# Gate and up projection of a SwiGLU part turned channel-major, in an encoder layer on one Trainium2 core

## The chip, the core and the metric

The kernel runs on one core of one Trainium2 chip. The metric is the time of one execution on the device, in microseconds. The engines are named TensorE (PE in the rows, PEld for its weight loads), VectorE (DVE), ScalarE (ACT), GpSimd (POOL) and SyncE (SP, which starts most DMAs).

## What is computed

One layer of a bidirectional encoder: 272 tokens (16 learned ones before 256) of width 2048 go through four token mixers, fed by one combined input projection, and then through a SwiGLU feed-forward part with 5632 hidden channels. The change is in the feed-forward part, for the 256 tokens that are kept:

```python
def rms_norm(x, gain):
    y = xf * lax.rsqrt(jnp.mean(xf * xf, axis=-1, keepdims=True) + EPS)
    return (y * gain.astype(F32)).astype(x.dtype)

def swiglu(n, w_gate, w_up, w_down):
    return (jax.nn.silu(n @ w_gate) * (n @ w_up)) @ w_down
...
        h = h + swiglu(rms_norm(h, norm_ffn[l]), ffn_w_gate[l], ffn_w_up[l], ffn_w_down[l])
    return rms_norm(h, norm_final)[:, N_META:]
```

All inputs are float32. The kernel splits each operand of a large product into a high part, which the faster matmul type of float32 holds, and the low part that is left; a product is then three matmuls: high by high, high by low, low by high.

## The kernel before

The work is a long run of matmuls over weights that stream in once. Every weight piece is 128 partitions of 1024 numbers (512 KB). `piece` (line 131) starts its DMA from SP into one of four `raw` buffers, lets ScalarE write the high part `hi` (line 152) and VectorE the low part `lo` (line 155), each into one of three buffers. The order of the pieces is the order in which the host has packed them (`pack`, line 1191).

There are two forms of matmul, named here by which operand is held in the array.

- `xs_gemm` (line 164) holds the tokens: 128 tokens by 128 input channels are the weights of the array, and 512 output channels of a weight piece move. Its results lie with tokens on the partitions: two accumulators (one for each 128 tokens) of 512 channels. A piece is 2 row blocks of 128 by 512 columns, and a piece does 12 matmuls (lines 178 to 180).
- `mix_chunk` (line 355), in the mixing part of the program, holds the weights: 128 by 128 of a piece are held and 272, 258 or 256 tokens move. Its results lie with channels on the partitions: two accumulators (one for each 128 channels). A piece is 4 row blocks by 256 columns, and does 24 matmuls (lines 364 to 366).

Both take their accumulators from one pool of four (`accp`).

The feed-forward part starts after the output projection. There, for each quarter `d` of the channels, `turn` (line 1034) transposes the residual stream `hh` on TensorE, ScalarE writes `n2h` and VectorE `n2l`: the input with channels on the partitions, times the norm's gain. The norm's other factor, one number per token (`rstd`), isn't in it: `sumsq` and `norm` (lines 1018, 1022) make it beside, and it is multiplied in behind the gate and up products. Work of this kind is put into a list `later`, and a product that starts emits the list after its first pieces: after 24 matmuls in the gate product (`at=4`, line 1058).

The hidden channels are done in 11 parts of 512, in two halves of 6 and 5 (`GU_HALF`): 6 parts, 1 part of the second half, the down product of the first half (`down(0, ...)`), the 4 other parts, the down product of the second. `gate_up` (line 1057) does a part: two `xs_gemm` calls, for each 128 tokens a silu with `rstd` as the scale on ScalarE (line 1070) and a product on VectorE (line 1071) that takes the up result times `rstd` times the silu. Tokens are on the partitions there, so `rstd` is one number per partition. The down product wants the hidden channels on the partitions, so each 128 by 512 result is transposed by 4 matmuls with the identity (line 1064, out of `later` in the product that follows), and `split` (line 199) makes `hidh` on ScalarE and `hidl` on VectorE out of it.

The order of each engine's queue is set by the framework's scheduler, from the order of the code, its own estimate of times and a priority that draws the preparation of pieces ahead.

Of the kernel before, what the change touches and what calls it, by code (L numbers as in the profile page):

```python
# [10 lines left out]
F32 = mybir.dt.float32  # L11
F32R = mybir.dt.float32r
U8 = mybir.dt.uint8
AF = mybir.ActivationFunctionType
# [3 lines left out]
P = 128  # L18
D = 2048
SEQ = 256  # L20
# [5 lines left out]
KT = D // P  # L26
# [4 lines left out]
GU_HALF = (6, 5)  # L31
# [38 lines left out]
def body(tc, a, out):  # L70
    nc = tc.nc
    V, G, A, PE = nc.vector, nc.gpsimd, nc.scalar, nc.tensor
    MUL, ADD, SUB = ALU.mult, ALU.add, ALU.subtract
# [7 lines left out]
    accp = pool("acc", 4, space=PSUM)  # L81
    psp = pool("ps", 4, space=PSUM)

    def ps(name="ps", shape=(P, 512)):
        return psp.tile(list(shape), F32, tag="ps", name=name)
# [7 lines left out]
    ident = const.tile([P, P], F32, name="ident")  # L93
# [37 lines left out]
    def piece(kt, cols, dst=None, skip=0):  # L131

        beside()
        i = wpos[0]
        wpos[0] += 1
        with tc.high_priority(offset=WAHEAD if i >= 6 else 0):
            raw = rawp.tile([P, kt, cols], F32, tag="raw", name="raw")
            nc.sync.dma_start(raw, a["w"][i].rearrange("p (k n) -> p k n", k=kt))
            if dst:
                hi, lo = dst  # L140
            else:
                hi, lo = [p.tile([P, 1024 + WPAD], F32R, tag=x, name=x)[:, skip:skip + 1024]
                          .rearrange("p (k n) -> p k n", k=kt) for p, x in ((hip, "hi"), (lop, "lo"))]
            if i < NPOOL:
                for j in range(kt):
                    ins = G.tensor_scalar(hi[:, j], raw[:, j], 1.0, 0.0, op0=MUL, op1=ADD)  # L146
                    if "G" in last:
                        after(ins, last["G"])
                    ins = G.tensor_tensor(lo[:, j], raw[:, j], hi[:, j].bitcast(F32), op=SUB)  # L149
                    last["G"] = ins  # L150
            else:
                ins = A.copy(hi, raw)  # L152
                if i in behind:
                    after(ins, behind[i][0])
                ins = V.tensor_tensor(lo, raw, hi.bitcast(F32), op=SUB)  # L155
                if i in behind:
                    after(ins, behind[i][1])
            if i == 1:
                first.append(ins.ins)
        return hi, lo  # L160

    later = []

    def xs_gemm(xh, xl, kts, at=2):


        acc = [accp.tile([P, 512], F32, tag="acc", name=f"acc{t}") for t in range(2)]
        n = len(kts)
        for i in range(0, n, 2):
            if i == at:  # L170
                while later:
                    later.pop(0)()
            wh, wl = piece(2, 512)
            for j in range(2):
                k = kts[i + j]
                for t in range(2):
                    s = slice(t * P, t * P + P)
                    PE.matmul(acc[t], xh[:, k, s], wh[:, j], start=(i + j == 0), stop=False)  # L178
                    PE.matmul(acc[t], xh[:, k, s], wl[:, j], start=False, stop=False)  # L179
                    PE.matmul(acc[t], xl[:, k, s], wh[:, j], start=False, stop=(i + j == n - 1))  # L180
        return acc
# [17 lines left out]
    def split(hi, lo, src):  # L199
        A.copy(hi, src)  # L200
        V.tensor_sub(lo, src, hi.bitcast(F32))

    def rsqrt(dst, ssum, scale):

        V.tensor_scalar(dst, ssum, scale, EPS, op0=MUL, op1=ADD)
        A.activation(dst, dst, AF.Sqrt)
        V.reciprocal(dst, dst)
# [5 lines left out]
    def half(name):  # L213
        return gp.tile([P, 512], F32, tag="half", name=name)
# [55 lines left out]
    def quarter(g, q):  # L270
        return xts[g][q // 2][:, q % 2 * 512:q % 2 * 512 + 512]
# [25 lines left out]
    for t in range(2):  # L297
        for q, e in enumerate("AVAV"):
            dump = H("dump", 512)
            x, acc = quarter(t, q), ss[:, t, q:q + 1]  # L300
# [21 lines left out]
    for k in range(KT):  # L322
        pt = ps("ptn")
        for t in range(2):
# [3 lines left out]
                                         op0=MUL, op1=SUB)]  # L328
# [683 lines left out]
    n2h = np_.tile([P, KT, SEQ], F32R, tag="nh", name="n2h")  # L1012
    n2l = np_.tile([P, KT, SEQ], F32R, tag="nl", name="n2l")
    ssum = const.tile([P, 2, 2, 4], F32, name="ssum")
    rstd = const.tile([P, 2, 2], F32, name="rstd")
    hh = {}

    def sumsq(i, t, d):
        dump = half("dump")
        A.activation(dump, hh[t, d], AF.Square, accum_out=ssum[:, i, t, d:d + 1])  # L1020

    def norm(i):
        V.tensor_reduce(rstd[:, i], ssum[:, i], op=ADD, axis=mybir.AxisListType.X)
        rsqrt(rstd[:, i], rstd[:, i], 1.0 / D)

    for d in range(4):
        acc = xs_gemm(mth, mtl, range(KT))
        for t in range(2):
            h = half("h")
# [16 lines left out]
        later.extend([lambda d=d: turn(d, 0), lambda d=d: turn(d, 1)])  # L1046
        for t in range(2):
            later.append(lambda t=t, d=d: sumsq(0, t, d))
    later.append(lambda: norm(0))
    ph1.close()  # L1050


    hid_p = pool("hid")
    hidh = [hid_p.tile([P, 4 * n, SEQ], F32R, tag=f"hid{i}h", name=f"hidh{i}") for i, n in enumerate(GU_HALF)]
    hidl = [hid_p.tile([P, 4 * n, SEQ], F32R, tag=f"hid{i}l", name=f"hidl{i}") for i, n in enumerate(GU_HALF)]

    def gate_up(part, c):
        ag = xs_gemm(n2h, n2l, range(KT), at=4)
        au = xs_gemm(n2h, n2l, range(KT))

        def turn(t, s):
            pt = ps("pth")
            for j in range(4):
                PE.transpose(pt[:, j * P:j * P + P], s[:, j * P:j * P + P], ident)  # L1064
            o = (slice(None), slice(4 * c, 4 * c + 4), slice(t * P, t * P + P))
            split(hidh[part][o], hidl[part][o], pt.rearrange("p (k n) -> p k n", k=4))

        for t in range(2):
            s = half("silu")
            A.activation(s, ag[t], AF.Silu, scale=rstd[:, 0, t:t + 1])  # L1070
            V.scalar_tensor_tensor(s, au[t], rstd[:, 0, t:t + 1], s, op0=MUL, op1=MUL)
            later.append(lambda t=t, s=s: turn(t, s))

    def add(acc, t, d, last):
        V.tensor_tensor(hh[t, d], acc, hh[t, d], op=ADD)
# [28 lines left out]
        for d in (0, 1, 2, 3):  # L1104
            (A if d == 2 else nc.sync).dma_start(out[t, d], hh[t, d])

    for c in range(GU_HALF[0]):
        gate_up(0, c)
    gate_up(1, 0)
    down(0, range(4))  # L1110
    for c in range(1, GU_HALF[1]):
        gate_up(1, c)
    nf = pool("nf").tile([P, D], F32, name="nf")
    G.dma_start(nf, a["norm_final"].partition_broadcast(P))
# [3 lines left out]
    part = const.tile([P, 2], F32, name="part")  # L1118
# [3 lines left out]
    n = 2 * GU_HALF[1]  # L1122
# [5 lines left out]
    for t in range(2):  # L1128
        acc = accp.tile([P, 512], F32, tag="acc", name="last")
        s = slice(t * P, t * P + P)  # L1130
        for k in range(2 * n):
            wh, wl = held[k // 2 * 2][:, k % 2], held[k // 2 * 2 + 1][:, k % 2]
# [58 lines left out]
def pack(inp):  # L1191
    inp = {k: np.asarray(v) for k, v in inp.items()}
# [4 lines left out]
    def rows(w, kt):  # L1197

        g = w.shape[0] // (P * kt)
        ws.append(w.reshape(g, kt, P, w.shape[1]).transpose(0, 2, 1, 3).reshape(g, P, kt * w.shape[1]))  # L1200
# [25 lines left out]
        rows(inp["w_out"][0][:, d * 512:d * 512 + 512], 2)  # L1226

    def w_gu(c):
        rows(inp["ffn_w_gate"][0][:, c * 512:c * 512 + 512], 2)
        rows(inp["ffn_w_up"][0][:, c * 512:c * 512 + 512], 2)  # L1230

    def w_down(part):
        r0 = 0 if part == 0 else 512 * GU_HALF[0]
# [35 lines left out]
    for d in range(2):  # L1269
        for w in range(NW):  # L1270
            for j, nm in enumerate(("lru_wa", "lru_wx")):
                for h in range(2):
                    s = slice(64 * h, 64 * h + 64)
# [29 lines left out]
```

## Time and profile before

| | us |
|---|---|
| median of 3 runs | 1685.68 (1684.83 to 1686.63) |
| the profiled execution | 1686.48 |
| its span in the profile | 1684.7 |
| TensorE busy in the span | 1662.2 (99%) |
| VectorE, ScalarE, GpSimd busy | 959.3 (57%), 795.0 (47%), 78.7 (5%) |
| DMA moved | 313.29 MB, 186 GB/s mean |

The busy share of an engine is the time in which at least one of its instructions is recorded; matmuls overlap in the array, so the mean duration of one is longer than the time from the start of one to the start of the next. The feed-forward part runs from 948.1 us to the end of the span.

### The profile page before, as it was taken

The page shows a single profiled execution, that of the slowest core. Times are in us where ns is not written, and L with a number is a line of the kernel's source. Part 1 is how long each engine was busy: PE and PEld are TensorE (multiplying, and loading weights), DVE is VectorE, ACT ScalarE, POOL GpSimd, SP SyncE. Part 2 cuts the span into 40 slices and gives each one's busy share as a digit, 9 for nine tenths or more (in the row PEclk, how much of TensorE's full clock was granted, in tenths as well). Part 3 has the DMA queues.
Part 4 walks back from the last instruction along what each step waited for, and adds up shares of the span by engine and source line. Part 5 has one row for each costly group of instructions (what it writes and reads, how often), then busy time and mean ns, then how long its engine had stood idle before and what let it go on. Part 6 is the DMA issues. An engine that isn't in the chain of part 4 may idle for free.

```text
span 1684.7 us, 22423 instructions
## 1 busy us (share of the span) xinstructions
PE 1662.2 (99%) x8856; PEld 1433.9 (85%) x8856; DVE 959.3 (57%) x1151; ACT 795.0 (47%) x967; POOL 78.7 (5%) x82
## 2 busy tenths in 40 slices
PE   8999999999999999999999999999999999999998
PEld 7999999988977888888888888888888888888886
DVE  6787865765767455464465545554455444455554
ACT  5654545754573444444444544444444334444444
POOL 3000000010002001020020000000000000000000
PEclk9999999999999999999999999999999999999999
DMA  6545555464545555555655555555555555555554
GB/s 239 182 140 176 161 176 176 154 217 156 176 137 196 192 193 192 189 198 189 203 199 200 199 190 189 191 193 188 189 191 190 191 196 192 189 190 192 191 188 150
DMA packets 87241, 313.29 MB, mean 186 GB/s; under 512 B 9840, under 2 KB 10256, under 8 KB 87008
## 3 DMA queue, kind: packets, MB, share of 16 engines
q1 hardware_dynamic: 84816, 303.90, 54.3%
q0 software_dynamic: 2032, 7.44, 1.4%
q8 instruction: 69, 1.13, 0.3%
q10 hardware_dynamic: 288, 0.52, 0.1%
q14 instruction: 36, 0.29, 0.0%
HBM read 308.65 MB, written 2.10 MB: 184 GB/s over the span
## 4 chain that ended last, share of the span: by engine, by line
PE 91%; DVE 3%; issue 2%; ACT 1%; DMA 1%; POOL 1%; SPq 0%; ACTq 0%; DVEq 0%
PE acc L180 23%; PE acc L179 23%; PE acc L178 23%; PE mix L366 5%; PE mix L365 5%; PE mix L364 5%; DVE lo L155 1%; PE pth L1064 1%; DMA raw<-in_w_dram 1%; PE last L1136 1%; PE last L1135 1%; PE last L1134 1%; DMA rot<-ck 0%; POOL lo L149 0%; PE pg L909 0%
## 5 line engine op out<-in xcount | busy, mean ns | idle before, releaser
L155 DVE TENSOR_TENSOR lo<-raw,hi 128x1024 fp32r<-128x1024 f32 x556 | 686.1, 1235 | 643.3 <-ACT hi L152 642.9
L152 ACT CAST hi<-raw 128x1024 fp32r<-128x1024 f32 x556 | 584.9, 1052 | 746.4 <-PE acc L180 619.4
L180 PE MATMUL acc<-hi,n2l 128*128 128x512 f32 x704 | 273.9, 389 | 0.0
L179 PE MATMUL acc<-lo,n2h 128*128 128x512 f32 x704 | 273.9, 389 | 0.0
L366 PE MATMUL mix<-nh,lo 128*128 128x272 f32 (+2 forms) x896 | 251.5, 284 | 2.3 <-DVE lo L155 1.9
L365 PE MATMUL mix<-nl,hi 128*128 128x272 f32 (+2 forms) x896 | 252.8, 284 | 0.0
L364 PE MATMUL mix<-nh,hi 128*128 128x272 f32 (+2 forms) x896 | 250.6, 284 | 0.3 <-POOL hi L146 0.3
L178 PE MATMUL acc<-hi,n2h 128*128 128x512 f32 x704 | 249.4, 390 | 0.0
L179 PE MATMUL acc<-lo,nh 128*128 128x512 f32 x512 | 200.8, 392 | 0.9 <-DVE lo L155 0.9
L180 PE MATMUL acc<-hi,nl 128*128 128x512 f32 x512 | 200.1, 391 | 0.0
L178 PE MATMUL acc<-hi,nh 128*128 128x512 f32 x512 | 183.5, 391 | 0.0
L366 PEld LDWEIGHTS mix<-nh,lo 128*128 128x128 f32 x896 | 167.4, 188 | 4.0 <-DVE lo L155 2.5
L365 PEld LDWEIGHTS mix<-nl,hi 128*128 128x128 f32 x896 | 168.6, 188 | 1.2 <-DVE nl L327 0.6
L364 PEld LDWEIGHTS mix<-nh,hi 128*128 128x128 f32 x896 | 167.5, 188 | 1.2 <-POOL hi L146 0.7
L180 PEld LDWEIGHTS acc<-hi,n2l 128*128 128x128 f32 x704 | 132.1, 188 | 27.5
L179 PEld LDWEIGHTS acc<-lo,n2h 128*128 128x128 f32 x704 | 132.2, 188 | 27.1
L178 PEld LDWEIGHTS acc<-hi,n2h 128*128 128x128 f32 x704 | 132.2, 188 | 27.1
L180 PE MATMUL acc<-hi,hidl 128*128 128x512 f32 x312 | 121.4, 389 | 0.0
L179 PE MATMUL acc<-lo,hidh 128*128 128x512 f32 x312 | 121.4, 389 | 0.0
L179 PEld LDWEIGHTS acc<-lo,nh 128*128 128x128 f32 x512 | 96.1, 188 | 21.8 <-DVE lo L155 2.2
L178 PEld LDWEIGHTS acc<-hi,nh 128*128 128x128 f32 x512 | 96.0, 188 | 20.2 <-ACT hi L152 0.3
L180 PEld LDWEIGHTS acc<-hi,nl 128*128 128x128 f32 x512 | 96.1, 188 | 19.5
(408 smaller groups left out, 1645.5 us busy)
## 6 DMA issues: line engine op xcount, KB each, us to landing
raw<-in_w_dram SPq DMA_DIRECT2D x568, 512.0 KB, 3.3
x<-in_x_dram SPq DMA_DIRECT2D x4, 512.0 KB, 7.9
h<-in_x_dram SPq DMA_DIRECT2D x8, 256.0 KB, 4.2
out_dram<-h SPq DMA_DIRECT2D x6, 256.0 KB, 2.3
lruw<-in_lruw_dram POOLq DMA_DIRECT2D x2, 512.0 KB, 5.0
dm<-in_decay_dram POOLq DMA_DIRECT2D x4, 256.0 KB, 4.6
nf<-in_norm_final_dram POOLq DMA_DIRECT2D x1, 1024.0 KB, 5.7
rot<-ck POOLq DMA_DIRECT2D x2, 272.0 KB, 6.8
```

Source lines behind the costliest of these rows:

```text
L152: ins = A.copy(hi, raw)
L155: ins = V.tensor_tensor(lo, raw, hi.bitcast(F32), op=SUB)
L178: PE.matmul(acc[t], xh[:, k, s], wh[:, j], start=(i + j == 0), stop=False)
L179: PE.matmul(acc[t], xh[:, k, s], wl[:, j], start=False, stop=False)
L180: PE.matmul(acc[t], xl[:, k, s], wh[:, j], start=False, stop=(i + j == n - 1))
L364: PE.matmul(o, wh[:, j, s], nh[:, k, t0:T], start=(k == 0), stop=False)
L365: PE.matmul(o, wh[:, j, s], nl[:, k, t0:T], start=False, stop=False)
L366: PE.matmul(o, wl[:, j, s], nh[:, k, t0:T], start=False, stop=(k == KT - 1))
L1064: PE.transpose(pt[:, j * P:j * P + P], s[:, j * P:j * P + P], ident)
L1134: PE.matmul(acc, xh, wh, start=(k == 0), stop=False)
L1135: PE.matmul(acc, xh, wl, start=False, stop=False)
L1136: PE.matmul(acc, xl, wh, start=False, stop=(k == 2 * n - 1))
```

## The change

Gate and up are computed in the other form: weights held, 256 tokens moving. A part is now 256 hidden channels (22 of them). `mix2` is the product: as `mix_chunk`, for the feed-forward input. Its results have channels on the partitions and tokens along the free axis, so nothing is transposed behind them, and `split` reads the product directly. The norm's factor is now a number per column: `rows` spreads it into a tile `rrow` of 128 equal rows, by a product of a matrix of ones with the diagonal matrix of `rstd`. It comes out of `later`, behind the transposes of the last normed rows, after 48 matmuls of the first gate product. Per part VectorE multiplies the two gate accumulators by `rrow`, ScalarE does one silu of 512 columns, VectorE multiplies the two up accumulators by the silu and then all by `rrow`. The host packs gate and up in pieces of 4 row blocks by 256 columns.

```diff
-    later.append(lambda: norm(0))
+    def rows():
+
+        norm(0)
+        pr = ps("prow")
+        for t in range(2):
+            diag = half("diag")[:, :P]
+            V.tensor_scalar(diag, ident, rstd[:, 0, t:t + 1], None, op0=MUL)
+            PE.matmul(pr[:, t * P:t * P + P], ones, diag, start=True, stop=True)
+        A.copy(rrow, pr[:, :SEQ])
+
+    later.append(rows)
...
+    ones = hid_p.tile([P, P], F32, name="ones")
+    G.memset(ones, 1.0)
+
+    def mix2(at):
+
+        acc = [accp.tile([P, SEQ], F32, tag="acc", name=f"acc{c}") for c in range(2)]
+        for q in range(4):
+            if q == at:
+                while later:
+                    later.pop(0)()
+            wh, wl = piece(4, 256, skip=16)
+            for j in range(4):
+                k = 4 * q + j
+                for c in range(2):
+                    s = slice(c * P, c * P + P)
+                    PE.matmul(acc[c], wh[:, j, s], n2h[:, k], start=(k == 0), stop=False)
+                    PE.matmul(acc[c], wh[:, j, s], n2l[:, k], start=False, stop=False)
+                    PE.matmul(acc[c], wl[:, j, s], n2h[:, k], start=False, stop=(k == KT - 1))
+        return acc
+
+    rrow = hid_p.tile([P, SEQ], F32, name="rrow")
 
     def gate_up(part, c):
-        ag = xs_gemm(n2h, n2l, range(KT), at=4)
-        au = xs_gemm(n2h, n2l, range(KT))
-
-        def turn(t, s):
-            pt = ps("pth")
-            for j in range(4):
-                PE.transpose(pt[:, j * P:j * P + P], s[:, j * P:j * P + P], ident)
-            o = (slice(None), slice(4 * c, 4 * c + 4), slice(t * P, t * P + P))
-            split(hidh[part][o], hidl[part][o], pt.rearrange("p (k n) -> p k n", k=4))
-
-        for t in range(2):
-            s = half("silu")
-            A.activation(s, ag[t], AF.Silu, scale=rstd[:, 0, t:t + 1])
-            V.scalar_tensor_tensor(s, au[t], rstd[:, 0, t:t + 1], s, op0=MUL, op1=MUL)
-            later.append(lambda t=t, s=s: turn(t, s))
+        ag = mix2(2)
+        s = half("silu").rearrange("p (c n) -> p c n", c=2)
+        for i in range(2):
+            V.tensor_tensor(s[:, i], ag[i], rrow, op=MUL)
+        A.activation(s, s, AF.Silu)
+        au = mix2(1)
+        for i in range(2):
+            V.tensor_tensor(s[:, i], au[i], s[:, i], op=MUL)
+        V.tensor_tensor(s, s, rrow[:, None, :].to_broadcast([P, 2, SEQ]), op=MUL)
+        split(hidh[part][:, 2 * c:2 * c + 2], hidl[part][:, 2 * c:2 * c + 2], s)
...
-    for c in range(GU_HALF[0]):
+    for c in range(2 * GU_HALF[0]):
         gate_up(0, c)
-    gate_up(1, 0)
+    for c in range(2):
+        gate_up(1, c)
     down(0, range(4))
-    for c in range(1, GU_HALF[1]):
+    for c in range(2, 2 * GU_HALF[1]):
         gate_up(1, c)
...
-        rows(inp["ffn_w_gate"][0][:, c * 512:c * 512 + 512], 2)
-        rows(inp["ffn_w_up"][0][:, c * 512:c * 512 + 512], 2)
+        for h in range(2 * c, 2 * c + 2):
+            rows(inp["ffn_w_gate"][0][:, h * 256:h * 256 + 256], 4)
+            rows(inp["ffn_w_up"][0][:, h * 256:h * 256 + 256], 4)
```

How the scheduler orders the queues shows at three places. The first is TensorE in the middle of a part, in the program before, where the hidden tiles of the part before are transposed (`pth`, 8 matmuls in a row) between the matmuls of the gate product:

```order
L180 MATMUL acc_9067<-hi,n2l 128x512
L1064 MATMUL pth<-ident,silu 128x128 x8
L178 MATMUL acc_9066<-hi,n2h 128x512
L179 MATMUL acc_9066<-lo,n2h 128x512
L180 MATMUL acc_9066<-hi,n2l 128x512
```

The change has no row of line 1064's kind any more: 88 instructions are gone from TensorE's queue, and the 2112 around them are 4224 of 128x256.

The second is TensorE in the first gate product of the changed program, from the transposes of the last normed rows (`pt`) to the last quarter of the input rows (`acc_8745` and `acc_8746` are the gate's accumulators, `acc_8905` and `acc_8906` those of the up product):

```order
L1039 MATMUL pt_8807<-ident,h 128x128 x4
L1039 MATMUL pt_8816<-ident,h 128x128 x4
...
L1081 MATMUL acc_8745<-n2h,hi 128x256
L1056 MATMUL prow<-diag,ones 128x128 x2
L1082 MATMUL acc_8745<-n2l,hi 128x256
...
L1081 MATMUL acc_8746<-n2h,hi 128x256
L1081 MATMUL acc_8905<-n2h,hi 128x256
L1082 MATMUL acc_8905<-n2l,hi 128x256
L1081 MATMUL acc_8906<-n2h,hi 128x256
```

The two matmuls that make `rrow` stand 13 matmuls behind the transposes, and matmuls of the up product have moved in between those of the gate product's last quarter.

The third is VectorE from there on. Before, with the product of line 1071 behind 13 pieces:

```order
L207 RECIPROCAL rstd<-rstd 128x2
L155 TENSOR_TENSOR lo<-raw,hi 128x1024
L1044 SCALAR_TENSOR_TENSOR n2l<-pt_8780,par,n2h 128x256
...
L155 TENSOR_TENSOR lo<-raw,hi 128x1024 x13
L1071 SCALAR_TENSOR_TENSOR silu<-acc_8914,rstd,silu 128x512
L1071 SCALAR_TENSOR_TENSOR silu<-acc_8915,rstd,silu 128x512
L155 TENSOR_TENSOR lo<-raw,hi 128x1024 x3
L201 TENSOR_TENSOR hidl_8739<-pth,hidh_8737 128x4x128 x2
```

and in the change:

```order
L207 RECIPROCAL rstd<-rstd 128x2
L1055 TENSOR_SCALAR diag<-ident,rstd 128x128 x2
...
L1092 TENSOR_TENSOR silu<-acc_8745,rrow 128x256
L1092 TENSOR_TENSOR silu<-acc_8746,rrow 128x256
L155 TENSOR_TENSOR lo<-raw,hi 128x1024 x4
L1096 TENSOR_TENSOR silu<-acc_8905,silu 128x256
L1096 TENSOR_TENSOR silu<-acc_8906,silu 128x256
L1097 TENSOR_TENSOR silu<-silu,rrow 128x512
L155 TENSOR_TENSOR lo<-raw,hi 128x1024
L201 TENSOR_TENSOR hidl_8739<-silu,hidh_8737 128x512
L155 TENSOR_TENSOR lo<-raw,hi 128x1024 x3
```

VectorE now meets an accumulator twice in every 8 pieces, where it met one once in 16. When it comes to a row of line 1092 or 1096, the low parts of two pieces beyond that product are done.

## Rows read from the trace of the kernel before

**Rows 1.** The page: busy time of TensorE, its busy tenths in 40 slices of the span, and its granted clock in tenths.

```profile
PE 1662.2 (99%) x8856; PEld 1433.9 (85%) x8856; DVE 959.3 (57%) x1151; ACT 795.0 (47%) x967; POOL 78.7 (5%) x82
...
PE   8999999999999999999999999999999999999998
...
PEclk9999999999999999999999999999999999999999
```

**Rows 2.** Busy time of each engine in three stretches of the feed-forward part: 6 parts, the first down product, 4 parts. Columns: stretch, its length, then per engine busy us and number of instructions, granted clock, share and GB/s of DMA.

```profile
core 0: us, PE busy (x) PEld busy (x) DVE busy (x) ACT busy (x) POOL busy (x), PEclk, DMA share, GB/s
...
948.10:1264.00 315.90, 315.90 (x1424) 262.14 (x1423) 159.04 (x149) 140.43 (x151) 0.00 (x0) 1.00 0.58 190
1264.00:1400.00 136.00, 136.00 (x605) 112.72 (x604) 66.45 (x61) 53.83 (x52) 0.00 (x0) 1.00 0.57 191
1400.00:1573.00 173.00, 173.00 (x781) 143.63 (x780) 86.00 (x77) 73.73 (x77) 0.00 (x0) 1.00 0.57 191
```

**Rows 3.** Groups of instructions by line, engine and shape, from 948.1 to 1677 us. Columns: count, then busy us of the group and mean ns of one, then the engine's idle time before them and what ended it.

```profile
L180 PE MATMUL acc<-hi,n2l 128*128 128x512 f32 x704 | 273.9, 389 | 0.0
L179 PE MATMUL acc<-lo,n2h 128*128 128x512 f32 x704 | 273.9, 389 | 0.0
...
L178 PE MATMUL acc<-hi,n2h 128*128 128x512 f32 x704 | 249.4, 390 | 0.0
...
L1071 DVE SCALAR_TENSOR_TENSOR silu<-acc,rstd,silu 128x512 f32<-128x512 f32 x22 | 15.4, 743 | 0.0
...
L201 DVE TENSOR_TENSOR hidl<-pth,hidh 128x512 fp32r<-128x512 f32 x22 | 14.1, 683 | 1.6 <-ACT hidh L200 1.6
...
L1064 PE MATMUL pth<-ident,silu 128*128 128x128 f32 x88 | 11.4, 272 | 0.0
```

**Rows 4.** TensorE in order of time, in the first part (start us, recorded duration us). Between two of these rows stand 12 matmuls.

```profile
959.91 0.61 PE L178 MATMUL acc<-hi,n2h 128*128 128x512 f32 x2
...
962.63 0.61 PE L178 MATMUL acc<-hi,n2h 128*128 128x512 f32 x2
...
970.79 0.61 PE L178 MATMUL acc<-hi,n2h 128*128 128x512 f32 x2
```

**Rows 5.** TensorE in order of time, around a group of transposes of hidden tiles.

```profile
997.76 0.39 PE L180 MATMUL acc<-hi,n2l 128*128 128x512 f32 x1
997.99 1.03 PE L1064 MATMUL pth<-ident,silu 128*128 128x128 f32 x8
998.78 0.48 PE L178 MATMUL acc<-hi,n2h 128*128 128x512 f32 x1
999.10 0.40 PE L179 MATMUL acc<-lo,n2h 128*128 128x512 f32 x1
999.33 0.39 PE L180 MATMUL acc<-hi,n2l 128*128 128x512 f32 x1
```

**Rows 6.** The chain of waits in order of time (start us, us): two groups of transposes, one part apart.

```profile
1042.57 0.87 PE pth L1064 x8
1086.98 0.87 PE pth L1064 x8
```

**Rows 7.** TensorE in order of time in the mixing part: first, second and last of 192 matmuls in a row of the form that holds the weights, with 256 tokens moving (two products of 96).

```profile
264.61 0.28 PE L364 MATMUL mix<-nh,hi 128*128 128x256 f32 x1
264.73 0.28 PE L365 MATMUL mix<-nl,hi 128*128 128x256 f32 x1
...
286.27 0.28 PE L366 MATMUL mix<-nh,lo 128*128 128x256 f32 x1
```

**Rows 8.** VectorE in order of time, around the end of the output projection. In brackets: idle time before, and what ended it.

```profile
943.98 1.22 DVE L155 TENSOR_TENSOR lo<-raw,hi 128x1024 fp32r<-128x1024 f32 x1 [1.49 <-ACT hi L152]
...
953.70 0.17 DVE L207 RECIPROCAL rstd<-rstd 128x2 f32<-128x2 f32 x1 [0.29 <-ACT rstd L206]
954.90 1.23 DVE L155 TENSOR_TENSOR lo<-raw,hi 128x1024 fp32r<-128x1024 f32 x1 [1.03 <-ACT hi L152]
956.04 0.87 DVE L1044 SCALAR_TENSOR_TENSOR n2l<-pt,par,n2h 128x256 fp32r<-128x256 f32 x2
957.07 0.88 DVE L1044 SCALAR_TENSOR_TENSOR n2l<-pt,par,n2h 128x256 fp32r<-128x256 f32 x2 [0.15 <-ACT n2h L1043]
```

**Rows 9.** Groups by line and shape over the whole span, columns as in rows 3: an elementwise product of two 128x512 tiles, and a 128x256 operation that reads an accumulator.

```profile
L718 DVE TENSOR_TENSOR ex<-ex,q 128x512 f32<-128x512 f32 x14 | 9.5, 681 | 0.0
...
L1094 DVE TENSOR_TENSOR h<-last,h 128x256 f32<-128x256 f32 x4 | 1.5, 419 | 11.8 <-PE last L1136 11.8
```

**Rows 10.** TensorE in order of time in the mixing part: first and last of 217 matmuls in a row with 272 tokens moving, and first and last of 6 with 258.

```profile
39.80 0.29 PE L364 MATMUL mix<-nh,hi 128*128 128x272 f32 x1
...
66.44 0.29 PE L364 MATMUL mix<-nh,hi 128*128 128x272 f32 x1
...
99.75 0.28 PE L364 MATMUL mix<-nh,hi 128*128 128x258 f32 x1
...
100.34 0.29 PE L366 MATMUL mix<-nh,lo 128*128 128x258 f32 x1
```

## Prediction

> **What bounds the kernel now.** I read the page first: TensorE is busy 99% of the span, in nearly every slice [rows 1]. Next the table of stretches over the feed-forward part, which the change touches: from 948.1 us on, TensorE is busy in every microsecond of the three stretches at a granted clock of 1.00, while VectorE stands at 50% (159.0 of 315.9 us) and ScalarE at 44% [rows 2]. So this stage lasts as long as the sum of its TensorE instructions, and another engine counts only if it makes TensorE wait, which now happens nowhere. Last the start-to-start times on TensorE, because busy time double-counts pipelined matmuls: a 512-wide matmul is listed with 389 ns [rows 3], yet 48 of them start in 970.79 - 959.91 = 10.88 us, or 226.7 ns each [rows 4]. All prices of matmuls below are such spacings.
>
> **What goes.** Per part of 512 hidden channels TensorE does 192 matmuls and 8 transposes; over 11 parts that is 2112 and 88 [rows 3]. A group of 8 starts at 997.99, where a matmul was due, and the next matmul starts at 998.78: 0.79 us. That first matmul then takes 999.10 - 998.78 = 0.32 us to the next start instead of 0.227: 0.09 more. So a group costs 0.88 us [rows 5]. The chain of waits confirms it from afar: two groups stand 1086.98 - 1042.57 = 44.41 us apart [rows 6], and 192 x 0.2267 = 43.52; the difference is 0.89. Eleven groups: **-9.8 us**. All of it lies on the path, as TensorE never idles there.
>
> **What is swapped.** 2112 matmuls of 512 columns become 4224 of 256 (22 half parts, two projections, 16 row blocks, 2 channel blocks, 3 products). The kernel before already does this form elsewhere, in its mixing projection: weights held, 256 tokens moving. There 192 matmuls in a row start between 264.61 and 286.27 us, across a change of accumulators and eight weight pieces, 21.66 / 191 = 113.4 ns each [rows 7]. Two of them are 226.8 against 226.7 for one 512-wide matmul. 4224 x 113.4 - 2112 x 226.7 = 479.0 - 478.8: **+0.2 us**. The doubled number of weight loads costs nothing there, since they run beside the matmuls, and I take the same here. This is the term on which the sum turns; its other bound comes under the rivals.
>
> **What is added on TensorE.** Two small fp32 matmuls that spread the norm's scale along the free axis. Nearest is a transpose, same tile and type: 0.1 us each and 0.1 for the change of kind behind them [rows 5]: **+0.3 us**. They sit in TensorE's queue, so everything behind waits if their input is late. By the order of the changed program they stand behind 48 matmuls, the 8 transposes of the normed rows and 13 matmuls: 948.13 + 5.44 + 0.88 + 1.47 = 955.9 us on the old time scale. Their input: the reciprocal of the norm starts at 953.70 and takes 0.17 [rows 8], then two scalings of a 128x128 tile, at most 0.42 each (the row of a tile twice as wide [rows 9]): 954.7 us. 1.2 us are left, so no wait. The memset of the ones on GpSimd is queued behind nothing late; GpSimd was idle from 948 to 1573 [rows 2].
>
> **What is brought forward.** In the first gate product the transposes of the last normed rows come after 48 matmuls of half the width, the same 5.4 us as before, but now the last quarter of the rows is wanted 24 half-width matmuls later. Before, 48 full-width ones (10.9 us) lay between. TensorE would get there at 957.4 us; the last n2l write ended at 957.07 + 0.88 = 957.95 [rows 8], and ScalarE now copies the scale row ahead of the last n2h, some 0.4 more. Bounds: 0, or the whole 958.4 - 957.4 = 1.0 us. I take 0: the queue puts 7 matmuls of the up product behind the first two of the last quarter, and the four row blocks are met one after another, the last at about 960.
>
> **VectorE and ScalarE.** Per 512 channels VectorE did two products of 743 ns and two splits of 683 [rows 3], 2.9 us. Now it does eight 128x256 products at 0.42 (nearest: 419 ns, also reading an accumulator), two 512-wide products at 0.68 [rows 9] and two splits: 6.1 us. The 3.2 us more per part of 43.5 lift it from 50% to about 57%. ScalarE keeps its number of silus and splits. Cost on the path: 0, under TensorE's 2.72 us per weight piece. The cover is a buffer: three pieces deep. When a projection ends, two pieces (5.44 us) lie ready; VectorE's queue then holds at most 0.84 + 0.68 us of products and 1.23 us of low part before the next piece is ready, 2.75 us. So 2.7 us are spare, in each of 44 places. Before, a wait of VectorE for ScalarE of 1.49 us per piece [rows 8] showed the same slack. DMA traffic is the same: the same 1024 numbers per partition and piece, in the same order on SP's queue. The accumulators still come in twos out of four, and each pair is read while the other is filled. Part results now come earlier, so down's first reads wait for nothing.
>
> **Sum:** -9.8 + 0.2 + 0.3 = -9.3 us. The profiled execution took 1686.5 (span 1684.7 and 1.8 around it), so 1677.2; the median of the runs, 1685.7, is 0.8 below it, so **1676.4 us** for the median. By the terms' bounds it is 1675 to 1678.
>
> **Rivals.**
> *A fixed price per matmul (slower).* If a matmul carries a piece that doesn't shrink with its width, doubling their number pays it 2112 times more. For it: 272-wide ones come at (66.44 - 39.80) / 216 = 123.3 ns and 258-wide ones at 0.59 / 5 = 118 [rows 10]. A line through 272 and 512 columns leaves 6.1 ns fixed and 116.4 ns at 256: 2112 x 6.1 = +12.9, in sum +3.4, 1689 us. At the 118 of the 258-wide row it is 2112 x 9.3 = +19.6, in sum +10.1, 1696. It decides from 115.6 ns on, where the change gives nothing. Against it: the 256-wide row itself, 113.4. What differs here is the tile that moves (rows of 256 apart instead of 320) and the weights' place. I give it 0.10.
> The Trainium skill, page TensorE: Matmul & The Clock Gate, section Back-to-back issue gap, states such a price: sustained 81 ns at 128 columns and 131 at 512 with a weight load each, and N/2.4 + 2.5 ns for one alone. An estimate from its sustained figures is 98 ns at 256, 64 more for two than for one 512-wide, +135 us; from the other formula 2.5 more, +5.3 us and 1681.7. The trace agrees with neither, as 226.7 and 113.4 are in the ratio of the widths.
> *The start of the part waits after all.* The scale matmuls or the last quarter hold TensorE for 1 to 3 us, once: 1678 to 1680 us. For it: both stand in TensorE's queue within 2 us of their inputs. Against it: the margins above. 0.10.
> *VectorE becomes late at each half part.* For it: its queue is in order, and the weights' low part now stands behind products that wait for an accumulator, 44 times. If it were 0.9 us late at each end of a half part: 22 x 0.9 = +20, in sum 1696. It costs only beyond the 2.7 spare microseconds; 0.04.
> That the transposes remain is out: the changed TensorE queue has none of the 88.
>
> **Chances.** Forecast 0.76, late start 0.10, fixed price 0.10, late VectorE 0.04. About 0.2% (3.4 us) is what a measurement of this kernel can tell from no change. The first two cases are faster: 0.86. Of the fixed price 0.04 falls within 0.2% (a small one), 0.06 beyond, with the late VectorE 0.10 slower. The range runs from 1674.5 (a microsecond below the sum's bounds, for the shift between profile and runs) to 1681.5, which holds the late start and a small fixed price and leaves out the slow cases.
>
> **What would show it.** Right: start-to-start 113.4 ns for 256-wide matmuls of the gate and up products; 21.8 us per half part; no transposes of hidden tiles; TensorE still busy all the time from 948 us on; VectorE at 55 to 60%. The start of the part has the two scale matmuls near 956 us with no idle time before. Wrong: spacing of 115 ns or more; idle time on TensorE behind VectorE's low parts at the ends of half parts, or before the last quarter of the first gate product.

## The result, and the profile after

The changed kernel takes 1694.58 us (median of 4 runs, 1693.36 to 1696.11) against 1685.69 (4 runs of the kernel before, 1684.83 to 1686.63): ratio 1.0055 [1.0043, 1.0067], **slower by 0.5%** where 0.5% faster was forecast. The profiled execution has a span of 1693.9 us; before it was 1684.7.

The page of the changed kernel: span, busy times, TensorE's tenths and its granted clock.

```profile
span 1693.9 us, 26618 instructions
...
PE 1671.2 (99%) x10884; PEld 1526.9 (90%) x10884; DVE 996.0 (59%) x1241; ACT 794.6 (47%) x968; POOL 79.0 (5%) x83
...
PE   8999999999999999999999999999999999999998
...
PEclk9999999999999999999999999999999999999999
```

The three stretches of [rows 2], with the same columns, now:

```profile
948.10:1264.00 315.90, 315.90 (x2685) 315.90 (x2684) 176.19 (x202) 138.78 (x151) 0.20 (x1) 1.00 0.56 186
1264.00:1400.00 136.00, 136.00 (x624) 113.57 (x623) 68.06 (x62) 53.08 (x52) 0.00 (x0) 1.00 0.57 193
1400.00:1573.00 173.00, 173.00 (x1471) 173.00 (x1470) 95.07 (x106) 72.89 (x77) 0.00 (x0) 1.00 0.56 187
```

Clock, busy share of TensorE, DMA share and the other engines are as forecast: TensorE never idles, VectorE stands at 176.19 / 315.9 = 56%. So no wait has come in; the stage is longer because the sum of TensorE's instructions is larger. How much, the last matmuls of the kernel show. Group by line of the `last` tile, before and after (min, median and max ns, then first and last start):

```profile
L1136 PE MATMUL last<-held,hidl x40: 388/389/389, 1645.4 to 1676.7; 128*128 128x512 f32 x40
```

```profile
L1163 PE MATMUL last<-held,hidl x40: 388/390/390, 1654.6 to 1685.9; 128*128 128x512 f32 x40
```

The part's first matmul starts at 948.13 before, as the prediction has it, and at 947.86 after, so from the first start to the last it is 728.6 us long before and 738.0 after: **+9.4**, the whole difference. Now the gate and up matmuls of the changed kernel on TensorE, in order of time: the first of all, then first two and last two of 2538 in a row (up to the first down product).

```profile
947.86 0.28 PE L1081 MATMUL acc<-n2h,hi 128*128 128x256 f32 x1
...
966.85 0.28 PE L1081 MATMUL acc<-n2h,hi 128*128 128x256 f32 x1
966.97 0.28 PE L1082 MATMUL acc<-n2l,hi 128*128 128x256 f32 x1
...
1265.54 0.28 PE L1082 MATMUL acc<-n2l,hi 128*128 128x256 f32 x1
1265.65 0.28 PE L1083 MATMUL acc<-n2h,lo 128*128 128x256 f32 x1
```

(1265.65 - 966.85) / 2537 = **117.78 ns** from start to start, where [rows 7] gave 113.4 for the same shape. A timeline row prints 0.28 us for both; only the mean durations of the groups in ns differ a little, 281 to 282 here against 276 there. 4.4 ns by 4224 is 18.6 us, against the 9.8 saved.

The start of the part, TensorE of the changed kernel in order of time:

```profile
953.52 1.03 PE L1039 MATMUL pt<-ident,h 128*128 128x128 f32 x8
954.31 0.36 PE L1081 MATMUL acc<-n2h,hi 128*128 128x256 f32 x1
...
955.93 0.61 PE L1056 MATMUL prow<-diag,ones 128*128 128x128 f32 x4
956.29 0.36 PE L1082 MATMUL acc<-n2l,hi 128*128 128x256 f32 x1
956.49 0.28 PE L1083 MATMUL acc<-n2h,lo 128*128 128x256 f32 x1
```

The scale matmuls come at 955.93 (forecast 955.9) with no idle time ahead. They show as four instructions for the two matmuls of the code, and take 956.29 - 955.93 plus 0.08 behind them: 0.44 us. VectorE of the changed kernel behind an up product (in brackets: idle before, and what ended it):

```profile
1016.88 0.78 DVE L1096 TENSOR_TENSOR silu<-acc,silu 128x256 f32<-128x256 f32 x2 [0.28 <-PE acc L1083]
1017.69 0.69 DVE L1097 TENSOR_TENSOR silu<-silu,rrow 128x512 f32<-128x512 f32 x1
1018.30 1.22 DVE L155 TENSOR_TENSOR lo<-raw,hi 128x1024 fp32r<-128x1024 f32 x1
1019.43 0.69 DVE L201 TENSOR_TENSOR hidl<-silu,hidh 128x512 fp32r<-128x512 f32 x1
1021.06 1.23 DVE L155 TENSOR_TENSOR lo<-raw,hi 128x1024 fp32r<-128x1024 f32 x1 [0.94 <-ACT hi L152]
```

VectorE does its products, a weight piece's low part (L155) and that of the hidden tile (L201) and is then idle for 0.94 us until ScalarE has the next high part: the slack that the forecast counted on is there.

### The profile page after: what moved, and what is told of

Same layout as the page of the kernel before. It is cut to its first block, busy times and chain, and to the rows that moved or that the text cites. A ratio compares the mean times of both kernels' runs of the same rounds, so it can differ in the third digit from the quotient of the medians.

```text
span 1693.9 us, 26618 instructions
## 1 busy us (share of the span) xinstructions
PE 1671.2 (99%) x10884; PEld 1526.9 (90%) x10884; DVE 996.0 (59%) x1241; ACT 794.6 (47%) x968; POOL 79.0 (5%) x83
## 4 chain that ended last, share of the span: by engine, by line
PE 82%; DVE 2%; issue 2%; ACT 1%; DMA 1%; POOL 0%; ACTq 0%; DVEq 0%
PE acc L180 14%; PE acc L179 14%; PE acc L178 14%; PE acc L1082 10%; PE acc L1083 10%; PE acc L1081 10%; PE mix L366 2%; PE mix L365 2%; PE mix L364 2%; DVE lo L155 1%; PE last L1163 1%; PE last L1161 1%; PE last L1162 1%; DMA rot<-ck 0%; PE pg L909 0%
## 5 line engine op out<-in xcount | busy, mean ns | idle before, releaser
L155 DVE TENSOR_TENSOR lo<-raw,hi 128x1024 fp32r<-128x1024 f32 x556 | 689.1, 1241 | 602.4 <-ACT hi L152 602.0
L1082 PE MATMUL acc<-n2l,hi 128*128 128x256 f32 x1408 | 396.0, 282 | 0.0
L1081 PE MATMUL acc<-n2h,hi 128*128 128x256 f32 x1408 | 395.7, 282 | 0.0
L1083 PE MATMUL acc<-n2h,lo 128*128 128x256 f32 x1408 | 395.6, 282 | 0.0
L1081 PEld LDWEIGHTS acc<-n2h,hi 128*128 128x128 f32 x1408 | 268.1, 191 | 0.1
L1082 PEld LDWEIGHTS acc<-n2l,hi 128*128 128x128 f32 x1408 | 266.8, 190 | 0.1
L1083 PEld LDWEIGHTS acc<-n2h,lo 128*128 128x128 f32 x1408 | 264.1, 188 | 0.0
```

What stands on the lines that cost most here:

```text
L1081: PE.matmul(acc[c], wh[:, j, s], n2h[:, k], start=(k == 0), stop=False)
L1082: PE.matmul(acc[c], wh[:, j, s], n2l[:, k], start=False, stop=False)
L1083: PE.matmul(acc[c], wl[:, j, s], n2h[:, k], start=False, stop=(k == KT - 1))
```

## The experiments

One question was left: why does the same form of matmul come at 113.4 ns in the mixing part and at 117.78 in gate and up? Three things differ between the places, or may: the accumulators' place, the distance between the moving rows, and the weights' place in their buffer (`skip` in `piece`, counted in numbers of 4 bytes; 16 in both). The first four runs put these to the test, and the transposes by themselves. Products (gate or up, 96 matmuls each, 44 in all) are counted from 0.

**Accumulators where the mixing part has them.**

```diff
-        acc = [accp.tile([P, SEQ], F32, tag="acc", name=f"acc{c}") for c in range(2)]
+        acc = [accp.tile([P, T], F32, tag="acc", name=f"acc{c}")[:, META:] for c in range(2)]
```

> The changed kernel, with one edit: the gate and up accumulators are columns 16 to 271 of a 272-column tile, as the 256-token products of the mixing part have them, instead of columns 0 to 255. In the changed kernel a 256-wide matmul of gate and up starts every 117.8 ns, in the mixing part every 113.4. Theory A (the place of the accumulator in its bank makes the difference): 113.4 ns here, 4224 x 4.4 = 18.5 us less than the changed kernel, about 1676 us. Theory B (the stride of the moving rows makes it) and theory C (the place of the weights): 117.8 ns as before, 1694.6 us.

Measured: 1693.93 against 1684.12, ratio 1.0055 [1.0038, 1.0072]; spacing 117.78. The accumulators' place is not it.

**Moving rows 320 apart, as in the mixing part.**

```diff
-    n2h = np_.tile([P, KT, SEQ], F32R, tag="nh", name="n2h")
-    n2l = np_.tile([P, KT, SEQ], F32R, tag="nl", name="n2l")
+    n2h = np_.tile([P, KT, LEAD + T], F32R, tag="nh", name="n2h")[:, :, LEAD + META:]
+    n2l = np_.tile([P, KT, LEAD + T], F32R, tag="nl", name="n2l")[:, :, LEAD + META:]
```

> The changed kernel, with one edit: the rows of the moving input (high and low part) stand 320 numbers apart and begin 64 numbers into the tile, as in the mixing part, instead of 256 apart from its start. Theory B (when all moving rows begin at the same place of a 1024-byte block they collide with the reads of the weights): 113.4 ns from start to start, about 1676 us. Theories A (accumulator's place) and C (weights' place): 117.8 ns, 1694.6 us.

Measured: 1693.57, ratio 1.0053 [1.0038, 1.0068]; 117.78 again. Not it either.

**Weights at the start of their buffer**, in gate and up and in the mixing part.

```diff
-            wh, wl = piece(4, 256, skip=16 if t0 else 0)
+            wh, wl = piece(4, 256, skip=0)
...
-            wh, wl = piece(4, 256, skip=16)
+            wh, wl = piece(4, 256, skip=0)
```

> The changed kernel, with one edit in two places: the weight tiles of gate and up, and those of all products of the mixing part, begin at the start of their buffer instead of 16 numbers in. Theory C (the distance between weights and moving rows matters, and another is right for gate and up): gate and up get faster than 117.8 ns while the 256-wide products of the mixing part (113.4 now) get slower, towards 118. Theories A and B: gate and up stay at 117.8; the mixing part's stay at 113.4 if the weights' place plays no part at all.

Measured: 1708.01, ratio 1.014 [1.0125, 1.0155]. Of this kernel, two rows 72 matmuls apart in a gate product:

```profile
1068.07 0.28 PE L1081 MATMUL acc<-n2h,hi 128*128 128x256 f32 x1
...
1076.71 0.28 PE L1081 MATMUL acc<-n2h,hi 128*128 128x256 f32 x1
```

8.64 / 72 = 120.0 ns, and the mixing part's 256-wide matmuls went from 113.4 to 120.0 too. So 64 bytes more or less in the weights' place change the spacing, by different amounts: 2.2 ns in gate and up, 6.6 in the mixing part. The place matters, but it doesn't explain why the same `skip` of 16 gives 117.78 in one part and 113.4 in the other.

**The kernel before without the 88 transposes.**

```diff
-            pt = ps("pth")
-            for j in range(4):
-                PE.transpose(pt[:, j * P:j * P + P], s[:, j * P:j * P + P], ident)
...
-            split(hidh[part][o], hidl[part][o], pt.rearrange("p (k n) -> p k n", k=4))
+            split(hidh[part][o], hidl[part][o], s.rearrange("p (k n) -> p k n", k=4))
```

> The kernel before, without the 88 transposes of the hidden tiles: the high and low parts of the hidden tiles are made from the untransposed products, so the down product works on wrong numbers of the right size. It measures the term of 9.8 us by itself. If the transposes lie wholly on the path: 1685.7 - 9.8 = 1675.9 us, and parts 43.5 us apart instead of 44.4. If something else takes their place (VectorE or ScalarE late with the weight pieces): between 1676 and 1685.7, with idle time on TensorE.

Measured: 1675.34 against 1684.12, ratio 0.9944 [0.9929, 0.9959]. First matmul of the part and the last group of this kernel:

```profile
945.73 0.39 PE L178 MATMUL acc<-hi,n2h 128*128 128x512 f32 x1
```

```profile
L1133 PE MATMUL last<-held,hidl x40: 388/389/389, 1633.2 to 1664.5; 128*128 128x512 f32 x40
```

The part is 1664.5 - 945.73 = 718.8 us long, 9.8 less than before. That term was right, and the account closes: -9.8 + 4224 x 4.44 ns (18.8) + 0.4 for the scale matmuls = +9.4.

**A map: each of the 44 products with another place.** The products go through `skip` 0, 16, 32, 48, 64 and four places of the accumulators in turn; once with moving rows 320 apart, once (without the edit of `n2h` and `n2l` above) 256 apart.

```diff
-        acc = [accp.tile([P, SEQ], F32, tag="acc", name=f"acc{c}") for c in range(2)]
+        skip, off = 16 * (len(calls) % 5), 16 * (len(calls) % 4)
+        calls.append(at)
+        acc = [accp.tile([P, SEQ + 64], F32, tag="acc", name=f"acc{c}")[:, off:off + SEQ] for c in range(2)]
...
-            wh, wl = piece(4, 256, skip=16)
+            wh, wl = piece(4, 256, skip=skip)
```

> A map in one run: the changed kernel with its moving rows 320 numbers apart and 64 in, as in the mixing part, where the 44 gate and up products of the feed-forward part take in turn five places of the weights in their buffer (0, 16, 32, 48, 64 numbers in) and four of the accumulator in its bank (0, 16, 32, 48 columns in), all 20 pairs twice. Neither the rows' stride nor the accumulator's place changed the 117.8 ns alone, while weights at 0 gave 120.0. Theory D (rows and accumulator only count together): the pair of 16 and 16, which is all that the mixing part has, gives 113.4 ns. Theory E (something outside the addresses of matmul and weights makes the difference to the mixing part): that pair gives 117.8 too, and the other places of the weights spread between 113 and 120 or more.

> The same map with the moving rows of the changed kernel, 256 numbers apart. Theory D: no pair gives 113.4 ns. Theory E: as the map with 320; the spacing depends on the weights' place alone, the same for all four places of the accumulator.

Measured, one run each: 1697.47 and 1696.93 against 1686.45. Both show the same pattern in spacing per product: `skip` 0: 120.0 ns; 32: 118.7; 48: 117.8; 64: 120.0; and 16: 113.3 in six products and 117.8 in three. The accumulators' place and the rows' distance change nothing. Of the kernel with rows 256 apart, two products with `skip` 16, in each two rows 72 matmuls apart:

```profile
1432.67 0.28 PE L1085 MATMUL acc<-n2h,hi 128*128 128x256 f32 x1
...
1441.15 0.28 PE L1085 MATMUL acc<-n2h,hi 128*128 128x256 f32 x1
...
1489.68 0.28 PE L1085 MATMUL acc<-n2h,hi 128*128 128x256 f32 x1
...
1497.84 0.28 PE L1085 MATMUL acc<-n2h,hi 128*128 128x256 f32 x1
```

8.48 / 72 = 117.8 and 8.16 / 72 = 113.3. With one setting there are two spacings, and each holds through a product. The products that came out of an even row of 120.0 ns settled at 117.8, those that came out of an uneven one (117, 121, 120, 124, 118 ns) at 113.3. That led to a new theory: at `skip` 16 the stream has **two steady rhythms**, and what comes before decides which one it falls into.

**A disturbance in each product**, of seven kinds, behind the sixth matmul (a row block of two channel blocks); `kick` is a tile that nobody reads.

```diff
+    def kick(kind, w, acc):
+
+        flat = n2h.rearrange("p k n -> p (k n)")
+        for n in ((), (64,), (64, 64), (128,), (16,), (272,), (512,), (64, 64, 64))[kind]:
+            PE.matmul(ps("kick")[:, 0:n], w, flat[:, 0:n], start=True, stop=True)
...
+        kind = (0, 1, 3, 2, 5, 4, 6, 7, 2, 3, 1, 6, 5, 7, 4, 3, 1, 5, 2, 7, 6, 4)[len(calls) % 22]
+        calls.append(at)
...
+                    if k == 1 and c == 0:
+                        kick(kind, wh[:, j, s], acc)
```

> The map showed that matmuls at the very same addresses run in one of two steady rhythms, 113.3 or 117.8 ns, and keep the one they fall into. Here all is as in the changed kernel, but each of the 44 gate and up products gets a disturbance near its start: an extra matmul whose result nobody reads, of 64, 128, 16, 272 or 512 columns, or two or three of 64. Theory F (two rhythms of the stream itself; an entry decides which): some disturbances switch the 117.8 ns to 113.3 for the whole product and the products after it, at unchanged addresses, buffers and neighbours on the other engines; others leave it or switch it back. Theory G (something that lasts, such as the traffic of the other engines or of the DMAs in this part, slows the matmuls): every product stays at 117.8 ns whatever is put before it.

Measured, one run: 1693.95 against 1685.83. Products that ran at 113.3 ns behind the disturbance, of all with that kind, by the spacing just ahead of it; the others ran at 117.8:

| columns | none | 16 | 64 | 64, 64 | 64, 64, 64 | 128 | 272 | 512 |
|---|---|---|---|---|---|---|---|---|
| from 113.3 | | 0 of 4 | | **3 of 3** | 0 of 4 | 0 of 5 | 4 of 4 | |
| from 117.8 | 0 of 2 | 2 of 2 | 1 of 6 | **3 of 3** | 2 of 2 | 1 of 1 | 0 of 2 | 4 of 6 |

Only two values come out. What a disturbance does depends on the rhythm that it meets: one matmul of 16, one of 128 and three of 64 columns turned it over in all 18 cases, and one of 272 left it in all 6. Two matmuls of 64 columns always gave the short one, from either; 64 alone and 512 met only the long one and gave both.

**Finer places.**

```diff
+        skip = (4, 8, 12, 20, 24, 28, 40, 56)[len(calls) % 8]
+        calls.append(at)
...
-            wh, wl = piece(4, 256, skip=16)
+            wh, wl = piece(4, 256, skip=skip)
```

> The changed kernel, where the 44 gate and up products take in turn finer places of the weights in their buffer: 4, 8, 12, 20, 24, 28, 40 and 56 numbers in (whole steps of 16 gave 120.0, 117.8 or 113.3, 118.6, 117.8 and 120.1 ns for 0, 16, 32, 48 and 64). Theory F says that the rhythm is a matter of how the reads of weights and moving rows mesh: the values lie between 113.3 and 120 with jumps between neighbours, and one of them may have 113.3 as its only rhythm, in all of its five or six products. Theory G: every place gives 117.8 or more.

Measured, one run: 1699.35 against 1685.83. In the order of the list: 118.3, 118.3, 117.8 (123.3 in the first of its six products), 118.8, 117.3 or 118.7, 119.9 or 120.1, 120.0, and 116.7. The hope for a place with 113.3 as its only rhythm failed; the expectation of 117.8 or more everywhere failed too, narrowly, at 56 and 24. No place among these reaches 113.3, so `skip` is not what to repair.

**Three disturbances in all**, of the kind that always worked, in products 2, 28 and 30; the first down product lies between products 27 and 28.

```diff
+        for n in (64, 64)[:kind]:
...
+        kind = 2 if len(calls) in (2, 28, 30) else 0
```

> The changed kernel with three disturbances in all: two extra matmuls of 64 columns, results unread, near the start of the third gate product, and of the first and second product after the first down product. In the kernel with a disturbance per product this one led to 113.3 ns in six of six, from either rhythm. Theory F (two rhythms, the stream keeps the one it falls into): 113.3 ns from there on through all further products of each stretch, without further help; of 4224 matmuls all but some 250 run 4.4 ns shorter: 17.6 us less, three disturbances at 0.25 us each more: 1694.6 - 16.9 = 1677.7 us, against 1685 of the kernel before a ratio of 0.995. A rival, theory H (the fast rhythm decays back to the slow one, as it needs the disturbance of every product): the spacing returns to 117.8 within some products, and the time lies between 1680 and 1694.

Measured, 5 runs: 1678.59 (1676.18 to 1679.06) against 1685.31 (1683.39 to 1687.03), ratio 0.9957 [0.9943, 0.997]: **faster than the kernel before**, and 16.0 below the changed kernel's median. TensorE of this kernel around the first disturbance, and 2483 matmuls further on the last of the row:

```profile
972.84 0.28 PE L1094 MATMUL acc<-n2l,hi 128*128 128x256 f32 x1
972.96 0.28 PE L1095 MATMUL acc<-n2h,lo 128*128 128x256 f32 x1
973.08 0.31 PE L1075 MATMUL kick<-n2h,hi 128*128 128x64 f32 x2
973.22 0.36 PE L1093 MATMUL acc<-n2h,hi 128*128 128x256 f32 x1
973.42 0.28 PE L1094 MATMUL acc<-n2l,hi 128*128 128x256 f32 x1
...
974.00 0.28 PE L1093 MATMUL acc<-n2h,hi 128*128 128x256 f32 x1
...
1255.41 0.28 PE L1095 MATMUL acc<-n2h,lo 128*128 128x256 f32 x1
```

Ahead of the two small matmuls the products run at 117.78 ns, behind them at 113.33, up to the down product at 1255.53: 26 products, with no decay within the row. Behind the down product, whose matmuls are 512 wide, it is gone:

```profile
1386.11 0.28 PE L1093 MATMUL acc<-n2h,hi 128*128 128x256 f32 x1
1386.23 0.28 PE L1094 MATMUL acc<-n2l,hi 128*128 128x256 f32 x1
1386.35 0.28 PE L1093 MATMUL acc<-n2h,hi 128*128 128x256 f32 x1
1386.46 0.28 PE L1094 MATMUL acc<-n2l,hi 128*128 128x256 f32 x1
1386.58 0.31 PE L1075 MATMUL kick<-n2h,hi 128*128 128x64 f32 x2
```

(1386.58 - 1386.11) / 4 = 117.5 ns. The disturbance in product 28 brings 113.33 back, and from there it holds to the last product; the one in product 30 found it in place. The end of the kernel:

```profile
L1175 PE MATMUL last<-held,hidl x40: 388/389/389, 1638.0 to 1669.3; 128*128 128x512 f32 x40
```

From its first matmul (948.43) the part is 720.9 us long, 7.7 less than before. The difference to the 9.3 of the forecast: two products at the long rhythm (192 x 4.44 ns = 0.85 us), three disturbances of 0.23 (973.08 to 973.42 is 0.34, where 0.11 were due) and 0.1 more for the scale matmuls.

**The cross test: the kernel before, with a disturbance in its mixing products.** If both rhythms belong to the form and not to gate and up, they must come out there too.

```diff
+                    if k == 1 and c == 0 and t0 == META:
+                        PE.matmul(ps("kick")[:, 0:P], wh[:, j, s], nh[:, 0, t0:t0 + P], start=True, stop=True)
```

> The kernel before with one extra matmul of 128 columns, result unread, near the start of each of the 12 products of the mixing part that move 256 tokens. In the changed kernel's stream this disturbance led from 113.3 to 117.8 ns in six of six. Theory F: the mixing part's 256-wide matmuls, 113.4 ns in the kernel before, fall into 117.8 ns behind it as well; at most 1152 x 4.4 = 5.1 us and 12 x 0.2 for the extra matmuls, 1691 to 1693 us where all lies on the path. Theory I (in the mixing part the fast rhythm is the only one, for a reason that the feed-forward part lacks): 113.4 ns again some ten matmuls behind each disturbance, at most 3 us more than the kernel before.

Measured, one run: 1690.18 against 1685.31. Five of the twelve disturbances met 113.3 and left 117.8, five met 117.8 and left 113.3, and two stand right behind 128-wide matmuls of another kind and left 113.3. So here too one matmul of 128 columns turns the rhythm over. (The count of six of six in the expectation is not right: in the run with seven kinds it was five of five from 113.3 to 117.8, and the sixth led from 117.8 to 113.3.) Here is TensorE of this kernel in the very products of [rows 7], around the second disturbance:

```profile
267.66 0.28 PE L368 MATMUL mix<-nh,lo 128*128 128x256 f32 x1
...
278.61 0.28 PE L368 MATMUL mix<-nh,lo 128*128 128x256 f32 x1
278.73 0.22 PE L365 MATMUL kick<-nh,hi 128*128 128x128 f32 x1
278.79 0.33 PE L366 MATMUL mix<-nh,hi 128*128 128x256 f32 x1
...
280.00 0.28 PE L367 MATMUL mix<-nl,hi 128*128 128x256 f32 x1
...
288.95 0.28 PE L368 MATMUL mix<-nh,lo 128*128 128x256 f32 x1
```

Between the disturbances 10.95 / 93 = 117.7 ns, behind the second 8.95 / 79 = 113.3. The first product of [rows 7], with its code and its place untouched but for the one matmul, has the gate product's spacing.

The kernel before shows the long rhythm without any disturbance too. Of its mixing part, in a product with `skip` 16, the last eighteen of twenty matmuls that follow a wait:

```profile
334.18 0.28 PE L364 MATMUL mix<-nh,hi 128*128 128x256 f32 x1
...
336.18 0.28 PE L366 MATMUL mix<-nh,lo 128*128 128x256 f32 x1
```

2.00 / 17 = 117.6 ns. In the run without transposes, where the mixing part is the same, these matmuls settle at 113.3.

## Why the prediction was wrong

- **What goes**: right. 9.8 us forecast, 9.8 measured with the transposes alone removed.
- **What is swapped**: this is the step that failed. It took 113.4 ns from [rows 7] as the price of the form, and 4224 of them as +0.2 us. The row was read rightly, but it was one of two values that the form has at this place of the weights; gate and up came out at 117.78, which makes the term 4224 x 117.78 - 2112 x 226.7 = +18.7 us. The trace of before held the other value as well, in the row at 334.18, and [rows 10] gave a hint with 118 for 258 columns, against which the text set the one row of 113.4. Its own sign of being wrong, a spacing of 115 ns or more, is what came.
- **The rival of a fixed price** had the sign and nearly the size (1696 at 118 ns), but not the mechanism. A piece that each matmul carries would not go away with two small matmuls ahead, and would be in [rows 7] as well. What the text named as differing there, the rows' distance and the weights' place, was tried: the first changes nothing, the second matters but is the same in both parts.
- The Trainium skill, page TensorE: Matmul & The Clock Gate, section Back-to-back issue gap, says that with a weight load for each matmul the spacing is set by the pipelined pair of both. The trace agrees that the pair counts: moving only the weights by 64 bytes took the spacing from 113.3 to 120.0 ns. Its sustained figures (81 ns at 128 columns, 131 at 512) match no row here: 512 columns come at 226.7 ns.
- **What is added**: 0.44 us instead of 0.3; the two matmuls show as four instructions. **What is brought forward**, and **VectorE and ScalarE**: right, no wait on TensorE, VectorE at 56% where 57% was forecast. So the late start and the late VectorE did not come.
- The chances were wrong with it: of the 0.10 for slower, 0.06 was for a fixed price and 0.04 for a late VectorE, and none for a form with two prices. One measured row of a form was taken for all of its future, and the range, 1674.5 to 1681.5, was drawn around that row and the small terms. The kernel with three disturbances lies in that range, with 1678.59.

Shown is that the form has two rhythms at one place of the weights, that what runs just before sets which, and that it holds as long as the row of 256-wide matmuls goes on. The traces also show where each part gets its own: in the five kernels that keep all of gate and up at `skip` 16 (the changed one, those with other accumulators or rows, with seven kinds and with three disturbances), the first gate product came at 117.8 right behind the 512-wide matmuls of the output projection, and the first behind the first down product too, 10 of 10. Mixing products at `skip` 16 that come right behind 272-wide matmuls (`skip` 0) fall to 113.3 within six matmuls, in the kernel before in 6 of 6. No run changed such an entry alone, so that the entry decides there is argued from these rows. Open is what in the array or its queue keeps a rhythm, and why an entry gives the one or the other.

## What to carry to other kernels

Before a price per matmul is carried to another place, look whether the trace has the form in more than one stretch, and take start-to-start times in each, since a timeline row prints 0.28 us in both rhythms. Here the trace of before had both. Where a long, gapless row of equal matmuls runs some ns above the same shape elsewhere, move its weights by 64 bytes and put a small matmul into it before blaming the form. Here a pair of unused matmuls of 64 columns, at 0.23 us, near the start of each of the two rows (and a third pair that was not needed) turned 0.5% slower into 0.4% faster; it rests on what ran before, so it has to be measured again after each change ahead of it.

## What was not expected of the hardware

- With weights loaded for each matmul and 256 columns moving, the spacing at granted clock 1.00 is 113.33 or 117.78 ns with nothing changed but a small matmul ahead. The short one held over 26 products and was gone behind the down product of 512-wide matmuls. A small matmul of 16 or 128 columns turned the rhythm over in 12 of 12 cases in gate and up, whichever it was. The group means of the recorded duration follow: 276 ns at 113.33, 281 to 282 at 117.78.
- The place of the weight tile in its buffer sets which spacings there are: 120.0 ns at 0 and 256 bytes, 113.3 or 117.8 at 64, 118.7 at 128, 117.8 at 192, 116.7 at 224. The Trainium skill, page SBUF — State Buffer, section A bandwidth-pool intuition that's wrong (but worth ruling out), lists an independent read port for weight loads; by that alone the place of the weights would not matter to the matmuls. In the runs it does matter: 64 bytes are worth up to 6.6 ns of 113.4. Whether the weight load itself is slower there, or one read holds up the other, they do not show.
- The moving rows' distance (256 or 320 numbers) and the accumulators' place (0 to 48 numbers) change nothing: 117.78 in each.
